# One hybrid decoder layer on one core: other part sizes in the third block's MLP, one norm at the end of the samples' attention, and a later place for the final norm's scaling

## The chip, the core and the metric

The kernel runs on one core of a Trainium2 chip. Time is device time in microseconds (us) of one execution, the median over the runs. A profile of one execution, taken by the hardware profiler, stands beside it: which instruction ran when on TensorE (PE, with its weight loads as PEld), VectorE (DVE), ScalarE (ACT), GpSimd (POOL), and what the DMA queue that SyncE (SP) issues did. In the profile's rows PEclk is the clock granted to TensorE, 1.00 being full speed.

## The reference

One inference step of one decoder layer, for a prompt of 2,048 tokens and for 64 sample tokens (8 sequences of 8, each with a paged cache of 2,048 past tokens), all in float32 with a model width of 1,024:

```
sh_m, sc_m, g_m, sh_f, sc_f, g_f = split(silu(c) @ w_ada + b_ada, 6)
h    = rmsnorm(x) * (1 + sc_m) + sh_m
rq, rk, rv, rg, sq, sk, sv = split(h @ w_in)        # 1024 -> 3584
ro   = groupnorm(retention(rotary(rq), rotary(rk), rv)) * silu(rg)   # 4 heads of 128
so   = stick_breaking_attention(sq, [past|sk], [past|sv])            # 8 heads of 64
so   = so * rsqrt(mean(so*so over each head) + eps) * sb_gn
x    = x + g_m * (concat(ro, so) @ w_out)
h    = rmsnorm(x) * (1 + sc_f) + sh_f
ff   = (silu(conv3(h @ w_up_gate)) * (h @ w_up_val)) @ w_down        # 1024 -> 2816 -> 1024
y    = rmsnorm_final(x + g_f * ff)
```

The outputs are y for prompt and samples, the new rows of k and v, the retention states and the last rows for the convolution.

## The kernel before

**Numbers.** Each float32 matrix product is done as three matmuls (L314, L315, L316) on a high and a low half of each operand, so that weights and activations are first split: an ACT cast writes the high half (L183, tile `whl` for weights, `act` for activations, `ahl` and `dmh` for attention results) and a DVE or POOL subtraction the low half (L165, which is the helper of all two-operand operations).

**Blocks.** The 2,048 tokens are worked in four blocks of 512, and each block in four tiles of 128. The 64 sample rows go with the fourth block (block number 3) through the MLP, as a fifth tile, which is then worked first. The MLP's inner width of 2,816 is 22 rows of 128.

**Stages.** First the modulation vectors; then the input projection of all four blocks, woven with the samples' attention (`decode`, L798 to L974); then the rest of the input projection with the samples' retention (`retention_sample`), the retention and the first block's attention; then, in the pool "mlp", the chain `mlps` (L1583): for each block `out_block` (output projection, residual, norm, and the `features` that bring the normed tiles into feature-major order, L1315) and then `ffn_block` (L1347). The attention of blocks 1 to 3 is woven into that chain. The last block's `ffn_block` runs alone, in the pool "mlp3".

**What sets the order.** The stages are Python generators. `_weave` takes the next step from the stream that is furthest behind its share of an assumed cost (1,230 for `mlps`, 420 for the attention there), so a moved `yield` moves work on every engine. A scheduler then orders the instructions of each engine; `tc.issue_after(x)` is a hint to it that what is issued under it comes after x. Small sets of buffers tie the engines together: six `whl` buffers (three pairs), two raw weight buffers, twelve `ff` buffers. The DMA loads and saves of all streams stand in one queue, SP's, in program order, and each waits there for its data or its buffer.

**The samples' attention, its end (L969 to L974).** `oT` holds the result as 4 x [128 features, 64 rows]. For each of the four, `sb_norm` (L450) squares it on ACT (L455), sums heads with small matmuls (L459), makes the reciprocal root in a chain of small POOL operations (tiles `sbr`, `sbms`), transposes it (L474), copies it out (L476), spreads it with a matmul against `sel4` (L479) and scales on DVE (L481). The result is split into `dmh`, of which there is one buffer, and saved to `mixs_sc` by one DMA each.

**The MLP (`ffn_block`, L1347).** It goes through `PARTS`, which are ranges of the 22 rows: 6, 6, 6 and 4. In each part the rows are made pair by pair (gate matmuls, a convolution of three taps, value matmuls, product, split into an `ff` tile), and then the part's share of the down projection is added, in two halves of 512 output columns. In the last part's second half two things are different. Ahead of it the next block's `out_block` is run (`after`, L1440). And the half's matmuls are done tile by tile (L1446 to L1456), with a step of the next block's `features` behind each tile, so that the matmuls of one tile cover the norm and modulation of the next block. Then come the weights of the next block's first gates, the residuals (L1459 to L1465) and `finish` (L1430), which is the final norm: square of the second half on ACT (L1432), reciprocal root on POOL (tile `rs_b`), scaling of one half on ACT (L1435) and of the other on DVE (L1436), and the DMA out. `finish` is a generator in two pieces, and a tile's second piece is called right behind the next tile's first.

## Time and profile before

| what | us |
|---|---|
| median of three runs | 3302.48 |
| the three runs | 3302.46, 3306.15, 3302.48 |
| the profiled execution | 3308.68 |
| span of the core in it, first to last instruction | 3307.0 |
| mean granted clock of TensorE in it | 0.986 |

| engine | busy us | share of the span | instructions |
|---|---|---|---|
| PE | 3187.8 | 96% | 17,879 |
| DVE | 2085.6 | 63% | 2,976 |
| ACT | 1580.0 | 48% | 2,796 |
| POOL | 1003.4 | 30% | 1,820 |

All stamps in the quoted rows are counted from the start of the span. A row of the wait view names the engine that waited, the tile and line that it was about to work on, and behind the arrow what ended the wait, then the total, the number of waits and the longest. A row of the window view gives for one stretch its length and the busy time (and number of instructions) of PE, PEld, DVE, ACT and POOL, then the granted clock, the share of the DMA engines and GB/s. A row of the groups gives busy time and mean ns of one instruction. A row of the timeline gives start, duration, engine, line and operation, and in brackets how long the engine had been idle and what released it.

### The profile page before, as it was taken

Reading aid. Unit: us, or ns where it says so; the run is one execution under the profiler, and the core shown is the slowest. Engines: PE = TensorE matmul, PEld = TensorE weight load, DVE = VectorE, ACT = ScalarE, POOL = GpSimd, SP = SyncE. Lnnn points to the kernel's source line nnn. Section 1 sums busy time; section 2 is a strip of 40 time slices with the busy share of each in tenths; the row PEclk is TensorE's granted clock in tenths of the full one; section 3 lists DMA queues with packets and bytes.
Section 4 is the critical chain, followed back from the end, with each engine's and each line's share of the span. In section 5 each row is a group of like instructions: output and inputs, shape, how many; then the busy total and the mean of one; then the engine's idle time right before and its main releaser. Section 6 shows DMA issues by size and latency. Waiting matters only on the chain. (4 is left out here: it accounts for less than half of the span.)

```text
span 3307.0 us, 50057 instructions
## 1 busy us (share of the span) xinstructions
PE 3187.8 (96%) x17879; PEld 2590.6 (78%) x17879; DVE 2085.6 (63%) x2976; ACT 1580.0 (48%) x2796; POOL 1003.4 (30%) x1820
## 2 busy tenths in 40 slices
PE   7999999999999989999999999999999999999998
PEld 5886777666878778878877778877788787799997
DVE  3345344245766587777778777787887874644445
ACT  4345335234534465545556555556655553533323
POOL 2012012013432243333344334344442433312112
PEclk8999999999999999999999999999999999999999
DMA  8757877785667744343454334354433335322321
GB/s 281 240 164 237 280 262 249 267 279 176 194 190 241 246 125 127 110 127 117 139 175 134 111 112 121 106 169 133 138 112 106 118 102 178 111 86 72 95 77 68
DMA packets 404135, 526.99 MB, mean 159 GB/s; under 512 B 25862, under 2 KB 242041, under 8 KB 403886
## 3 DMA queue, kind: packets, MB, share of 16 engines
q1 hardware_dynamic: 369966, 472.27, 45.6%
q10 hardware_dynamic: 33920, 51.52, 4.2%
q8 instruction: 142, 2.33, 0.3%
q14 instruction: 107, 0.88, 0.1%
HBM read 442.11 MB, written 81.60 MB: 158 GB/s over the span
## 5 line engine op out<-in xcount | busy, mean ns | idle before, releaser
L183 ACT CAST whl<-raw 128x1024 fp32r<-128x1024 f32 x408 | 427.6, 1050 | 1080.9 <-PE d L315 814.2
L165 DVE TENSOR_TENSOR whl<-raw,whl 128x1024 fp32r<-128x1024 f32 x408 | 521.6, 1280 | 571.8 <-ACT whl L183 561.6
L314 PE MATMUL d<-act,whl 128*128 128x512 f32 (+2 forms) x2016 | 742.9, 369 | 4.2 <-ACT whl L183 2.3
L316 PE MATMUL d<-act,whl 128*128 128x512 f32 (+2 forms) x2016 | 733.5, 364 | 0.0
L315 PE MATMUL d<-act,whl 128*128 128x512 f32 (+2 forms) x2016 | 731.4, 363 | 0.8 <-DVE act L165 0.8
L314 PEld LDWEIGHTS d<-act,whl 128*128 128x128 f32 x2016 | 382.8, 190 | 73.9 <-issue 12.0
L316 PEld LDWEIGHTS d<-act,whl 128*128 128x128 f32 x2016 | 382.1, 190 | 60.8 <-DVE whl L165 1.3
L315 PEld LDWEIGHTS d<-act,whl 128*128 128x128 f32 x2016 | 383.9, 190 | 55.8 <-DVE act L165 1.0
L314 PE MATMUL d<-whl,ff 128*128 128x512 f32 x704 | 279.6, 397 | 0.0
L315 PE MATMUL d<-whl,ff 128*128 128x512 f32 x704 | 278.7, 396 | 0.0
L316 PE MATMUL d<-whl,ff 128*128 128x512 f32 x704 | 278.1, 395 | 0.0
L314 PE MATMUL d<-whl,act 128*128 128x512 f32 x640 | 259.5, 407 | 4.0 <-ACT whl L183 4.0
L316 PE MATMUL d<-whl,act 128*128 128x512 f32 x640 | 258.3, 404 | 0.0
L315 PE MATMUL d<-whl,act 128*128 128x512 f32 x640 | 257.8, 403 | 0.0
L1181 DVE TENSOR_TENSOR_SCAN aom<-aom,acy 128x512 f32<-128x512 f32 x192 | 255.0, 1328 | 2.3 <-ACT aom L1167 1.7
L165 DVE TENSOR_TENSOR abe<-abe,aom 128x512 f32<-128x512 f32 (+2 forms) x320 | 230.5, 720 | 24.7 <-POOL abe L1171 2.5
L1205 PE MATMUL acc<-ahl,avv 128*128 128x512 f32 (+3 forms) x640 | 223.9, 411 | 12.0 <-DVE ahl L165 9.0
L1167 ACT ACTIVATE aom<-z,nb 128x512 f32<-128x512 f32 (+2 forms) x320 | 200.8, 628 | 62.8 <-PE z L1164 40.5
L1168 ACT ACTIVATE abe<-z,bb 128x512 f32<-128x512 f32 (+2 forms) x320 | 199.4, 623 | 0.7 <-DVE kf L165 0.7
L165 DVE TENSOR_TENSOR ahl<-z,ahl 128x512 fp32r<-128x512 f32 (+1 forms) x320 | 191.3, 598 | 10.9 <-ACT ahl L183 10.6
L1164 PE MATMUL z<-akk,aq 128*128 128x512 f32 (+3 forms) x640 | 190.1, 374 | 6.9 <-DVE ahl L165 3.1
L1374 DVE SCALAR_TENSOR_TENSOR c<-a,vecs,c 128x512 f32<-128x512 f32 x176 | 135.3, 769 | 80.8 <-ACT c L1371 46.1
(286 smaller groups left out, 5677.8 us busy)
## 6 DMA issues: line engine op xcount, KB each, us to landing
raw<-in_w_in SPq DMA_DIRECT2D x56, 1024.0 KB
raw<-in_w_up_gate SPq DMA_DIRECT2D x44, 1024.0 KB
raw<-in_w_up_val SPq DMA_DIRECT2D x44, 1024.0 KB
akk<-k SPq DMA_DIRECT2D x160, 256.0 KB
page<-in_cache_k_pages SPq DMA_DIRECT2D x128, 256.0 KB
vpage<-in_cache_v_pages SPq DMA_DIRECT2D x128, 256.0 KB
raw<-in_w_down SPq DMA_DIRECT2D x32, 1024.0 KB
raw<-in_w_ada SPq DMA_DIRECT2D x24, 1024.0 KB
```

Of the source, the lines that this page charges most:

```text
L165: eng.tensor_tensor(o, a, b, op)
L183: act.copy(hi, src)
L314: pe.matmul(ps, sh, mh, start=start, stop=False)
L315: pe.matmul(ps, sh, ml, start=False, stop=False)
L316: pe.matmul(ps, sl, mh, start=False, stop=stop)
L1164: pe.matmul(z[:, :n], qs[g, h][:, i * P : (i + 1) * P], kk[:, c, :n], start=c == 0, stop=c == 1)
L1167: act.activation(om[:, :n], z[:, :n], AF.Sigmoid, bias=nb[:, h : h + 1], scale=-SCALE)
L1168: act.activation(be[:, :n], z[:, :n], AF.Sigmoid, bias=bb[:, h : h + 1], scale=SCALE)
L1181: dve.tensor_tensor_scan(rv, rv, rv, init, ALU.mult, ALU.bypass)
L1205: pe.matmul(accs[0][:, cs], kv[u][1][:, kt, :], m[:, cs], start=(s == g and kt == 0 and c == 0), stop=(s == 0 and kt == NT - 1 and c == 1),)
L1374: dve.scalar_tensor_tensor(c[:, :TB], a[:, j : j + TB], cw(j), c[:, :TB], ALU.mult, ALU.add)
```

## The change

It has three parts. (1) The third block (number 2) gets parts of 6, 4, 4 and 8 rows instead of 6, 6, 6 and 4. The last part's second half begins with the rows but the last four, pair by pair over all tiles, with a step of `features` behind each pair, and does the last four rows tile by tile as before. For parts of four rows this loop is empty, so the other blocks keep their order. (2) At the end of the samples' attention one `sb_norm` over [128, 256] takes the place of four over [128, 64]: one square, two matmuls of the sums, two transposes, one copy, one `sel4` matmul, four scalings with a gain each, then one split into a `kh` tile and one DMA. (3) In `finish` the second piece of a tile is called two tiles behind, with the hint that it be issued behind the newest residual and square; the last two come behind the loop without a hint. This holds for all four blocks.

```
+LAST_PARTS = [(0, 6), (6, 10), (10, 14), (14, 22)]
...
-    def sb_norm(o, n, pl, gain, tag, rtag="sbsq", wait=0):
+    def sb_norm(o, n, pl, gains, tag, rtag="sbsq", wait=0, stag="sbsq"):
...
-        dve.scalar_tensor_tensor(out, o, gain, pb[:, :n], ALU.mult, ALU.mult)
+        w = n // len(gains)
+        for i, gain in enumerate(gains):
+            cs = slice(i * w, i * w + w)
+            dve.scalar_tensor_tensor(out[:, cs], o[:, cs], gain, pb[:, cs], ALU.mult, ALU.mult)
...
-        for j in range(4):
-            m = yield from steps(sb_norm(oT[:, j, :], NS, dp, vecs[:, V_SG + j : V_SG + j + 1], "dm"), 0.2)
-            mh = T(dp, [P, 2, NS], F32R, "dmh")
-            split(mh[:, 0], mh[:, 1], m)
-            sv(mixs_sc[4 + j], mh)
+        gains = [vecs[:, V_SG + j : V_SG + j + 1] for j in range(4)]
+        m = yield from steps(
+            sb_norm(oT.rearrange("p j t -> p (j t)"), 4 * NS, dp, gains, "aT", "aT", stag="aT"), 0.8
+        )
+        mh = T(dp, [P, 4, 2, NS], F32R, "kh")
+        split(mh[:, :, 0], mh[:, :, 1], m.rearrange("p (j t) -> p j t", j=4))
+        sv(mixs_sc[4:].rearrange("j p c n -> p j c n"), mh)
...
-        tt(eng, x2[:n, cs], x2[:n, cs], tmp[:n], ALU.add)
+        return eng.tensor_tensor(x2[:n, cs], x2[:n, cs], tmp[:n], ALU.add)
...
-                    wts = list(w_tm(w_dn, f0, f1 - f0, half * 512))
+                    wts = w_tm(w_dn, f0, f1 - f0, half * 512)
+                    for _ in range(f0, f1 - 4, 2):
+                        q0, w = next(wts)
+                        for q in range(2):
+                            for tile in ordered:
+                                one(pss, tile, f0 + q0 + q, w, q)
+                        yield cost / 2
+                        next(feats, None)
+                    wts = list(wts)
...
-                        residual(pss[tile[0]], gfs[half][tile[0] == NT], x2[tile[0]], half, tile[2], fp, dve)
+                        added = residual(pss[tile[0]], gfs[half][tile[0] == NT], x2[tile[0]], half, tile[2], fp, dve)
                         ends.append(finish(*tile, nf))
-                        next(ends[-1])
-                        if len(ends) > 1:
-                            next(ends[-2], None)
-                    next(ends[-1], None)
+                        squared = next(ends[-1])
+                        if len(ends) > 2:
+                            with tc.issue_after(added.ins), tc.issue_after(squared.ins):
+                                next(ends[-3], None)
+                    for end in ends[-2:]:
+                        next(end, None)
...
-                st = (yield from ffn_block(g, st, fp, False, nxt))[0]
+                st = (yield from ffn_block(g, st, fp, False, nxt, LAST_PARTS if g == 2 else PARTS))[0]
```

Lines behind the new constant move by one (L165 becomes L166, L183 becomes L184), and the residual's addition gets a line of its own (L1352); the scaling on DVE goes from L1436 to L1442.

Three places of the program show what moves. First SP, which issues the loads and saves, at the end of the samples' attention: `ms<-dmh` are the saves of the four norms' results, `raw` weights of the input projection, `rot` the rotary table, and the last four rows are loads of the retention stage behind. Before:

```order
L171 DMA raw_10078<-in_w_in 128x4x512
L171 DMA ms_148<-dmh_9643 128x128
L171 DMA rot_10485<-in_rot 128x2x512
L171 DMA raw_10221<-in_w_in 128x4x512
L171 DMA ms_148<-dmh_9670 128x128
L171 DMA ms_148<-dmh_9697 128x128
L171 DMA ms_148<-dmh_9758 128x128
L171 DMA c_decs_9797<-in_con 64x256
L171 DMA rv_9799<-rvs_114 64x512
L171 DMA rg_9801<-rgs_115 64x512
L171 DMA sqT_9804<-rqs_112 128x64
```

and now:

```order
L172 DMA raw_10002<-in_w_in 128x4x512
L172 DMA rot_10409<-in_rot 128x2x512
L172 DMA raw_10145<-in_w_in 128x4x512
L172 DMA ms_148<-kh_9682 128x4x128
L172 DMA c_decs_9721<-in_con 64x256
L172 DMA rv_9723<-rvs_114 64x512
L172 DMA rg_9725<-rgs_115 64x512
L172 DMA sqT_9728<-rqs_112 128x64
```

The saves, which stood between the weight loads and after them, have become one, `ms<-kh`, directly ahead of the retention's loads.

Second DVE between the third block's and the fourth block's MLP: `act<-hf` is the low half of a tile of the fourth block's features, `hf<-z` and `hf<-hf` their modulation, `whl<-raw` the low half of weights, `hf<-d` and `ff<-ff` the third block's residuals. Before:

```order
L165 TENSOR_TENSOR act_107_186<-hf_30639,act_107_186 128x4x128
L165 TENSOR_TENSOR whl_30735<-raw_30728,whl_30734 128x1024
L165 TENSOR_TENSOR act_107_186<-hf_30677,act_107_186 128x4x128
L165 TENSOR_TENSOR hf_30711<-z_30706,coef_102_168 128x512
L165 TENSOR_TENSOR hf_30711<-hf_30711,coef_103_169 128x512
L165 TENSOR_TENSOR whl_30943<-raw_30940,whl_30942 128x1024
L165 TENSOR_TENSOR act_107_186<-hf_30711,act_107_186 128x4x128
L165 TENSOR_TENSOR hf_30738<-d_30526,gp_25784 128x512
L165 TENSOR_TENSOR hf_30743<-d_30527,gp_25784 128x512
L165 TENSOR_TENSOR ff_24858<-ff_24858,hf_30738 128x512
L165 TENSOR_TENSOR ff_24861<-ff_24861,hf_30743 128x512
L165 TENSOR_TENSOR hf_30757<-d_30528,gp_25784 128x512
```

and now:

```order
L166 TENSOR_TENSOR whl_30651<-raw_30648,whl_30650 128x1024
L166 TENSOR_TENSOR act_107_186<-hf_30525,act_107_186 128x4x128
L166 TENSOR_TENSOR hf_30573<-z_30568,coef_102_168 128x512
L166 TENSOR_TENSOR hf_30573<-hf_30573,coef_103_169 128x512
L166 TENSOR_TENSOR act_107_186<-hf_30573,act_107_186 128x4x128
L166 TENSOR_TENSOR hf_30607<-z_30602,coef_102_168 128x512
L166 TENSOR_TENSOR hf_30658<-d_30388,gp_25708 128x512
L166 TENSOR_TENSOR hf_30607<-hf_30607,coef_103_169 128x512
L1352 TENSOR_TENSOR ff_24782<-ff_24782,hf_30658 128x512
L166 TENSOR_TENSOR hf_30663<-d_30389,gp_25708 128x512
L166 TENSOR_TENSOR act_107_186<-hf_30607,act_107_186 128x4x128
L1352 TENSOR_TENSOR ff_24785<-ff_24785,hf_30663 128x512
```

Before, the weights' low half stands ahead of the last tile's features and the residuals behind them; now two of the third block's residuals have moved in among the last two tiles' features.

Third DVE at the very end: `hf<-d` and `ff<-ff` are the residuals of the fourth block, and the rows that read `rs_b` are the final norm's scaling, of the samples (64x512) and of the four tiles. Before:

```order
L165 TENSOR_TENSOR hf_34809<-d_34717,gp_30802 128x512
L1436 SCALAR_TENSOR_TENSOR ff_34793<-ff_30234,rs_b_34803,gp_34714 64x512
L165 TENSOR_TENSOR ff_30225<-ff_30225,hf_34809 128x512
L1436 SCALAR_TENSOR_TENSOR ff_34798<-ff_30222,rs_b_34817,gp_34714 128x512
L165 TENSOR_TENSOR hf_34823<-d_34718,gp_30802 128x512
L1436 SCALAR_TENSOR_TENSOR ff_34812<-ff_30225,rs_b_34831,gp_34714 128x512
L165 TENSOR_TENSOR ff_30228<-ff_30228,hf_34823 128x512
L165 TENSOR_TENSOR hf_34837<-d_34719,gp_30802 128x512
L165 TENSOR_TENSOR ff_30231<-ff_30231,hf_34837 128x512
L1436 SCALAR_TENSOR_TENSOR ff_34826<-ff_30228,rs_b_34845,gp_34714 128x512
L1436 SCALAR_TENSOR_TENSOR ff_34840<-ff_30231,rs_b_34854,gp_34714 128x512
```

and now:

```order
L166 TENSOR_TENSOR hf_34720<-d_34637,gp_30722 128x512
L166 TENSOR_TENSOR hf_34734<-d_34638,gp_30722 128x512
L1352 TENSOR_TENSOR ff_30087<-ff_30087,hf_34720 128x512
L1442 SCALAR_TENSOR_TENSOR ff_34713<-ff_30096,rs_b_34728,gp_34634 64x512
L1352 TENSOR_TENSOR ff_30090<-ff_30090,hf_34734 128x512
L1442 SCALAR_TENSOR_TENSOR ff_34718<-ff_30084,rs_b_34742,gp_34634 128x512
L166 TENSOR_TENSOR hf_34748<-d_34639,gp_30722 128x512
L1442 SCALAR_TENSOR_TENSOR ff_34737<-ff_30090,rs_b_34765,gp_34634 128x512
L1352 TENSOR_TENSOR ff_30093<-ff_30093,hf_34748 128x512
L1442 SCALAR_TENSOR_TENSOR ff_34723<-ff_30087,rs_b_34756,gp_34634 128x512
L1442 SCALAR_TENSOR_TENSOR ff_34751<-ff_30093,rs_b_34774,gp_34634 128x512
```

Before, each scaling stands about one residual behind its own; now the residuals of the second and third tile stand ahead, with the samples' scaling between them, but the scaling of the third tile (`ff_34737`) is queued ahead of the last tile's addition, and that of the second tile behind it.

More of the change, by code (lines that the diff above doesn't have):

```diff
@@ L448, in to_features @@
             half_features(xs[kh], o, n, kh, A, B, acts[kh], hpool)
-    def sb_norm(o, n, pl, gain, tag, rtag="sbsq", wait=0):
+    def sb_norm(o, n, pl, gains, tag, rtag="sbsq", wait=0, stag="sbsq"):
         w = min(P, n)
         nt = n // w
-        sq = T(pl, [P, n], F32, "sbsq")
+        sq = T(pl, [P, n], F32, stag)
         act.activation(sq, o, AF.Square)
@@ L1218, in post @@
         def post(g, j, o2):
-            m = yield from sb_norm(o2, 512, tp, vecs[:, V_SG + j : V_SG + j + 1], "sbsq", *(("ahl", 1) if g else ()))
+            m = yield from sb_norm(o2, 512, tp, [vecs[:, V_SG + j : V_SG + j + 1]], "sbsq", *(("ahl", 1) if g else ()))
             mh = [T(tp, [P, 512], F32R, "ahl") for _ in range(2)]
@@ L1344, in residual, with ffn_block @@
         tt(dve, tmp[:n], fold(ps, n, fp)[:n], gate[:n, :], ALU.mult)
-        tt(eng, x2[:n, cs], x2[:n, cs], tmp[:n], ALU.add)
-    def ffn_block(g, x2, fp, samp, after=None):
+        return eng.tensor_tensor(x2[:n, cs], x2[:n, cs], tmp[:n], ALU.add)
+    def ffn_block(g, x2, fp, samp, after=None, parts=PARTS):
         t = TB + (NS if samp else 0)
@@ L1382, in gate @@
             return c
-        for f0, f1 in PARTS:
+        for f0, f1 in parts:
             ffs = {}
@@ L1431, in finish @@
                 y = T(fp, [P, 2 * t], F32, "ff")
-                act.activation(y[:n, :512], x2[i][:n, 512:], AF.Square, accum_out=ss[i][:n, 1:2])
-                yield
+                yield act.activation(y[:n, :512], x2[i][:n, 512:], AF.Square, accum_out=ss[i][:n, 1:2])
                 r = rows_rstd(ss[i], n)
@@ L1453, in ffn_block @@
                                 one(pss, tile, f0 + q0 + q, w, q)
-                        yield cost * (f1 - f0) / 4 / len(tiles)
+                        yield cost / len(tiles)
                         next(feats, None)
@@ L1544, in body @@
                 dict(smp=1, page=4, kh=4, vpage=6, aT=10, qsm=1, ksm=1, oT=1,
-                     tm=1, sbsq=1, dm=1, dmh=1, ptab=1, sbc=1, dbias=1, m8n=1, c_hm2=1, c_gsum=1),
+                     tm=1, ptab=1, sbc=1, dbias=1, m8n=1, c_hm2=1, c_gsum=1),
             )
```

## The prediction

> **What bounds the kernel now.** I read the page first, then the waits of TensorE, then the stretches around each place that the change touches.
>
> ```profile
> PE 3187.8 (96%) x17879; PEld 2590.6 (78%) x17879; DVE 2085.6 (63%) x2976; ACT 1580.0 (48%) x2796; POOL 1003.4 (30%) x1820
> PE   7999999999999989999999999999999999999998
> PEclk8999999999999999999999999999999999999999
> ```
>
> TensorE is busy 96% of the span, in every slice, and no other engine passes 63%. The change adds and removes almost no matmul work, so what it can win is the idle time of PE, 3307.0 − 3187.8 = 119.2 us in small gaps, and what else is lost where the granted clock is under 1. The three places touched are short stretches, so I cost each from its own window. All sums are made against the profiled execution, 3308.68 us (span 3307.0), which lies 6.2 above the median of 3302.48; since every term is a difference between two orders of the same work, I take the sum off the median unchanged. A measurement of this kernel tells some 0.2%, or 6.6 us, from nothing.
>
> **Part A, one norm at the end of the samples' attention.**
>
> ```profile
> PE z L474 <- POOL sbr L165: 2.8, 2, 1.5
> 744.00:747.00 3.00, 1.51 (x8) 0.90 (x7) 1.51 (x3) 1.15 (x2) 2.08 (x5) 1.00 0.02 9
> 747.00:757.00 10.00, 10.00 (x24) 6.16 (x25) 0.34 (x2) 0.66 (x3) 1.94 (x7) 0.51 0.34 112
> 757.00:767.00 10.00, 10.00 (x44) 8.02 (x43) 3.26 (x6) 3.57 (x6) 0.00 (x0) 0.98 0.19 56
> L479 PE MATMUL z<-sbsq,sel 4*128 4x64 f32 x4 | 1.4, 354 | 0.0
> L459 PE MATMUL z<-con,sbsq 128*64 128x2 f32 x8 | 1.2, 220 | 0.0
> L474 PE MATMUL z<-con,sbr 64*4 64x64 f32 x4 | 0.9, 227 | 2.8 <-POOL sbr L165 2.8
> ```
>
> The first row says that PE waited for the norms' POOL chain twice, 1.3 and 1.5 us. With one norm there is one such chain: the first wait stays, the second goes, 1.5 us. Behind the second wait the granted clock is 0.51 for ten microseconds (second window row), in which 24 matmuls were begun against 44 in the ten behind it. At the later rate these 24 take 24/44 × 10 = 5.5 us, so the slow stretch costs 4.5. I tie it to the second wait: PE was busy for half of the three microseconds ahead of it, and it begins where that thin stretch ends. The matmuls of the four norms take 1.4 + 1.2 + 0.9 = 3.5 us; one norm has one `sel4` matmul in place of four, two sums for eight and two transposes for four, so that some 1.5 are left and 2.0 go. Together 1.5 + 4.5 + 2.0 = **8.0 us**. Bounds: 3.5 if the clock falls anyway, and 9.4 if the first wait (1.3) goes too and 0.1 more of the norm's matmuls.
>
> What the new norm adds lies off PE, and the trace has no operation of just its size. The rows that bracket them:
>
> ```profile
> L455 ACT ACTIVATE sbsq<-o 128x512 f32<-128x512 f32 x16 | 10.1, 634 | 6.7 <-DVE o L165 6.6
> L455 ACT ACTIVATE sbsq<-oT 128x64 f32<-128x64 f32 x4 | 1.0, 257 | 7.0 <-DVE oT L934 4.0 <-PE z L479 3.0
> L479 PE MATMUL z<-ahl,sel 4*128 4x512 f32 x12 | 5.9, 493 | 0.0
> ```
>
> The square of 256 columns lies between 257 and 634 ns, and I take 0.38, between them in proportion. The `sel4` matmul lies between 354 and 493 ns, and I take 0.40. The wait that stays can thus grow by about 0.2 us, which I leave in the bounds. On SP the change goes past these:
>
> ```profile
> 746.76 16.02 SPq L171 DMA_DIRECT2D ms<-dmh  x3
> POOL km L1119 <- DMA sqT<-rqs: 15.8, 1, 15.8
> ```
>
> Three of the old saves blocked the queue for 16.02 us, because each needed the single `dmh` buffer, whose ACT casts stood behind a weight cast; POOL's first step of the retention stage waited 15.8 us for a load behind them. Now one save stands there, and those loads go some 15 us earlier. I cost this at nothing: PE has the input projection in hand meanwhile, in the window from 757 to 767 it is busy throughout, and that it goes on so is the cover; without it a rival (below) takes the 8 us back.
>
> **Part B, from the third block to the fourth.**
>
> ```profile
> PE z L314 <- ACT act L443: 5.1, 1, 5.1
> PE z L315 <- DVE act L165: 1.3, 1, 1.3
> PE z L420 <- DVE hf L165: 0.7, 1, 0.7
> PE z L420 <- ACT c L1324: 0.3, 1, 0.3
> 2860.00:2865.00 5.00, 0.07 (x1) 0.07 (x1) 4.97 (x6) 4.44 (x10) 1.84 (x2) 0.84 0.27 68
> 2865.00:2870.00 5.00, 3.69 (x14) 3.34 (x15) 5.00 (x7) 3.03 (x8) 1.87 (x4) 0.50 0.41 144
> 2870.00:2876.00 6.00, 6.00 (x46) 6.00 (x45) 3.29 (x6) 3.59 (x9) 3.25 (x8) 0.98 0.44 175
> 2842.64 0.40 PE L316 MATMUL d<-whl,act 128*128 128x512 f32 x1
> 2847.54 0.40 PE L316 MATMUL d<-whl,ff 128*128 128x512 f32 x1
> 2864.93 0.85 PE L314 MATMUL z<-act,whl 128*128 128x288 f32 x2 [5.08 <-ACT act L443]
> 2866.36 0.68 DVE L165 TENSOR_TENSOR act<-hf,act 128x512 fp32r<-128x512 f32 x1
> ```
>
> The first four rows are all the waits of PE from 2843 to 2876: 5.1 + 1.3 + 0.7 + 0.3 = 7.4 us. The first gate of the fourth block waits for the last tile's features. The 14 matmuls begun in the half-clock stretch (0.50) took 3.69 us; at the next row's 46/6 = 7.7 per us they take 1.8, so 1.9 more is lost. By the clock column the stretch at half lasts 0.16/0.5 × 5 + 5 + 0.02/0.5 × 6 = 6.8 us, and part A's 9.8 + 0.4 = 10.2: two and three steps of 3.4, in which I price such stretches. Now the cover. The features run as one chain from the last matmul of the output projection (2842.64) to the last split on DVE (2866.36 + 0.68 = 2867.04): 24.4 us. Against it PE has the half's matmuls and the transposes. From 2842.64 to 2847.54 are 21 steps of 0.233 us. Before, the last part has 4 rows × 4 tiles × 3 = 48 matmuls, 11.2 us; the features' transposes are what is left to 2864.93 − 5.08 = 2859.85: 17.2 less 11.2 less the small waits (1.0), 5.0. Now the part has 8 rows: 96 matmuls, 22.4 us, and 22.4 + 5.0 = 27.4 against 24.4. The gates then find their features, and 3.0 us are to spare. The extra 48 matmuls aren't added: they come out of the part of rows ahead of `out_block`. Of the waits I leave the 0.3 at the start: 7.4 − 0.3 + 1.9 = **9.0 us**. Bounds: 4 (if residuals that moved ahead of the last features on DVE delay them by as much as they spare, and the clock then falls for its 1.9) and 9.4.
>
> What these 48 matmuls leave behind is cover for the attention of the last block, whose end `out_block(3)` waits for:
>
> ```profile
> 2772.97 0.50 PE L479 MATMUL z<-ahl,sel 4*128 4x512 f32 x1
> 2776.86 0.34 SPq L171 DMA_DIRECT2D mx<-ahl  x1
> 2783.01 0.59 SPq L171 DMA_DIRECT2D smp<-ms  x1
> 2792.87 0.47 PE L323 MATMUL z<-whl,smp 128*128 128x512 f32 x1
> ```
>
> From the last `sel4` matmul to the save of its result on SP are 3.9 us, to the samples' load behind it 10.0, with its own 0.59 10.6; the samples' matmul came 19.9 behind. In the new order 24 matmuls (5.6 us, before 72) stand between that `sel4` matmul and the output projection, and the samples' matmuls come 34 matmuls further on: 14.0 us. So 14.0 against 10.6 is enough, and I cost it at nothing; the spare 3.4 us are about one weight load in SP's queue, and a rival has it.
>
> **Part C, the end.**
>
> ```profile
> 3296.34 0.75 DVE L1436 SCALAR_TENSOR_TENSOR ff<-ff,rs_b,gp 128x512 f32<-128x512 f32 x1 [1.20 <-POOL rs_b L165]
> 3298.34 0.69 DVE L165 TENSOR_TENSOR ff<-ff,hf 128x512 f32<-128x512 f32 x1
> 3300.02 0.75 DVE L1436 SCALAR_TENSOR_TENSOR ff<-ff,rs_b,gp 128x512 f32<-128x512 f32 x1 [1.00 <-POOL rs_b L165]
> 3302.57 0.75 DVE L1436 SCALAR_TENSOR_TENSOR ff<-ff,rs_b,gp 128x512 f32<-128x512 f32 x1 [1.80 <-POOL rs_b L165]
> 3300.65 0.61 ACT L1432 ACTIVATE ff<-ff 128x512 f32<-128x512 f32 x1
> 3301.43 0.19 POOL L165 TENSOR_TENSOR sst<-os 128x1 f32<-128x1 f32 x1 [1.45 <-ACT ff L1432]
> 3301.99 0.55 POOL L165 TENSOR_TENSOR rs_b<-rs_a,nhalf 128x1 f32<-128x1 f32 x1
> ```
>
> The last addition ends at 3299.03, but its square begins only at 3300.65, because ACT has the third tile's scaling queued ahead; square to scaling then takes 3300.65 to 3303.32. Two things win. The last addition comes earlier, since the second tile's scaling, which waited 1.20 and took 0.75, is no longer ahead of it; the third tile's still is, in the order shown above, so of this 1.95 I take 1.6: it ends near 3297.4. And its square follows at once, 0.8 with the read of its sum; POOL's chain (3301.43 to 3302.54) takes 1.1, the scaling 0.75, with small passages 2.9: 3300.3 instead of 3303.32. That is **3.0 us**; bounds 1.9 (one of the two) and 3.3.
>
> **Part D, the same rescheduling between blocks 0, 1 and 2.**
>
> ```profile
> PE acc L1205 <- DVE ahl L165: 1.6, 1, 1.6
> PE acc L1205 <- DVE ahl L165: 2.1, 1, 2.1
> ```
>
> These are the longest waits of PE from 1720 to 1790 and from 2290 to 2350: attention splits on DVE that stand behind a waiting scaling. If the scalings no longer wait there, 3.7 us go; something else will often be late next, so I take half, **2.0 us**, with bounds of 0 and 5.4 (3.7 and half of a clock step of 3.4).
>
> **Sum.** 8.0 + 9.0 + 3.0 + 2.0 = 22.0; 3308.68 − 22.0 = 3286.7, on the median 3302.48 − 22.0 = **3280.5 us**.
>
> **A rule weighed.** The row at 747 shows half clock behind a wait of 1.5 us. The Trainium skill, "TensorE: Matmul & The Clock Gate", sections "What's actually happening" and "HAM oscillation — how this bites in real kernels", says that the gate halves the clock after an idle window of some 3.4 us, in windows that run free of the program. By that rule a 1.5 us wait doesn't make the slow stretch, part A would be worth 3.5 and the sum 17.5. The trace agrees for B, where 5.1 us of wait stand ahead of the stretch, and speaks against it in A.
>
> **The rivals.**
>
> *The slow clock at 747 stays.* A thin stretch remains (fewer, but still dependent small matmuls and the wait of 1.3), and the clock falls behind that wait instead. A is 3.5: 3285.0. For it: the wait that stays is nearly as long as the one that goes (1.3 and 1.5). Against: before, behind the first wait the window from 744 still shows 1.00. Chance 0.14.
>
> *The output projection waits for the last attention row.* If a weight load (3.6 us) holds SP's queue between that row's saves, PE waits some 4 us ahead of the fourth block, and the clock falls for one or two steps of 3.4 us at half, 1.7 to 3.4. That takes 5.7 to 7.4 of B's 9.0: about 3288. For it: only 3.4 us to spare. Against: both saves are queued early. Chance 0.13.
>
> *A is given back.* The retention stage, whose loads come 15 us earlier, draws work on DVE and ACT forward, and the input projection's splits come later: the 8.0 goes, 3288.5. Chance 0.09. With the rival before it, 3288.5 + 7.4, about 3296: within 0.2%. Chance 0.05.
>
> *Slower, by the phase of the clock.*
>
> ```profile
> 1150.00:1200.00 50.00, 41.91 (x235) 35.69 (x236) 42.07 (x58) 34.46 (x69) 19.63 (x42) 0.86 0.38 110
> ```
>
> Here a clock of 0.86 means 0.14/0.5 × 50 = 14 us at half, 7 lost. Everything behind 745 moves by 8 us, and with it where each small gap lies against the steps of the clock. If gaps that now pass unpunished draw such stretches, each 7 us at worst, four take back 22 + 6.6 = 28.6: that is the point from which it is slower; five give 3302.5 − 22 + 35 = 3315.5. For it: most of the 119 us are small gaps. Against: as many stretches may vanish. Chance 0.03.
>
> **How the numbers follow.** The forecast has 0.56, the rivals 0.14, 0.13, 0.09, 0.05 and 0.03. Faster: 0.56 + 0.14 + 0.13 + 0.09 = 0.92; same 0.05; slower 0.03. Downward the range reaches 9.4 + 9.4 + 3.3 + 5.4 = 27.5 and some 2 of clock elsewhere: 3273. Upward it takes in the three faster rivals with 3 us for the bounds of C and D: 3292. Outside are the last two and little else.
>
> **What would show it.** Right: no second wait of the transposes of `sbr` near 745 and a clock near 1 from 747 to 757; one save there, and `km` no longer waiting; the first gate of the fourth block without a wait of its own above 1 us and no half clock behind it; the last square right behind the last addition, and the last scaling three microseconds nearer to it. Wrong: a new wait of `d` matmuls for `act` or `smp` loads ahead of the fourth block's output projection; the slow stretch still behind the single norm; or gaps in the retention stage that were not there.

## The result, and the profile after

| kernel | median us | runs | before beside it | ratio to before, 95% interval |
|---|---|---|---|---|
| changed | 3286.24 | 6 | 3305.95 | 0.9945 [0.9934, 0.9956] |
| changed, measured again (`after_again`) | 3284.13 | 6 | 3304.84 | 0.9933 [0.9910, 0.9956] |

The change makes the kernel faster, by 0.0055 × 3305.95 = 18.2 us in the first measurement and 0.0067 × 3304.84 = 22.1 in the second; 22.0 were forecast. In time, 3280.5 us were forecast and 3286.24 and 3284.13 measured; 3.5 and 2.4 us of that distance are there because before itself ran slower beside the change (3305.95 and 3304.84) than the 3302.48 from which the forecast was taken. The profiled execution took 3287.1 us with a span of 3285.4, 21.6 under that of before. First the page, its totals and clock:

```profile
PE 3175.4 (97%) x17870; PEld 2584.1 (79%) x17870; DVE 2084.3 (63%) x2970; ACT 1577.2 (48%) x2787; POOL 999.9 (30%) x1805
PEclk8999999999999999999999999999999999999999
```

PE is busy 12.4 us less, with nine matmuls fewer, and idle 110.0 us, 9.2 less. So more than half of what this trace gains isn't idle time: it is matmuls that don't run at half clock, and the norm's small ones. Not all of it is the change's, as the next table shows.

**Where it came from, stage by stage.** All kernels here split the same 408 weight pieces on DVE (`whl<-raw`). The start of the n-th split, counted from 0, is a milestone; the table has the time in the trace of before, and for each other trace how much later (earlier where negative) it is there. The end is that of the last scaling on DVE.

| milestone | before, us | changed | again | A only | B only | C only | `smp_first` | `best` |
|---|---|---|---|---|---|---|---|---|
| 78, ahead of the norms | 735.8 | -3.9 | -0.9 | -1.7 | -3.1 | -1.6 | +3.3 | -5.2 |
| 88, retention begun | 843.7 | -11.0 | -12.1 | -14.2 | -3.8 | -4.2 | -9.0 | -17.9 |
| 190, ahead of 0→1 | 1691.6 | -11.6 | -14.1 | -13.9 | -3.5 | -2.5 | -9.4 | -19.7 |
| 202, behind 0→1 | 1797.1 | -12.4 | -14.8 | -14.2 | -3.3 | -3.2 | -10.2 | -21.8 |
| 265, ahead of 1→2 | 2270.2 | -12.5 | -14.9 | -14.2 | -3.4 | -3.2 | -10.2 | -21.7 |
| 276, behind 1→2 | 2368.7 | -14.3 | -16.7 | -15.8 | -3.3 | -5.0 | -12.0 | -22.9 |
| 330, ahead of 2→3 | 2767.9 | -13.7 | -16.2 | -15.7 | -2.7 | -4.9 | -11.4 | -22.3 |
| 350, behind 2→3 | 2909.8 | -20.0 | -25.2 | -14.6 | -8.5 | -4.3 | -21.3 | -32.2 |
| 405, ahead of the end | 3262.2 | -20.0 | -25.1 | -14.6 | -8.5 | -4.3 | -21.2 | -32.1 |
| end | 3303.3 | -22.5 | -27.7 | -14.6 | -8.5 | -6.9 | -23.8 | -35.6 |

Two things are seen in it. Up to the first milestone every trace has the instructions of before in the same order, and yet they lie from -5.2 to +3.3 (`six_rows`, which the table leaves out, at -5.6): 8.9 us from one execution to another, as much as a term of the forecast, so only differences between milestones are read. And the time changes at the places of the change and moves by at most 2.0 us between them.

**A, the norm.** The waits of PE from 730 to 760, the two windows that stood at half clock and at full speed in before, and SP's save:

```profile
PE z L476 <- POOL sbr L166: 1.3, 1, 1.3
```
```profile
747.00:757.00 10.00, 10.00 (x51) 7.36 (x50) 3.07 (x5) 2.22 (x3) 1.12 (x3) 1.00 0.97 235
757.00:767.00 10.00, 9.34 (x50) 6.60 (x49) 4.86 (x10) 6.21 (x16) 2.58 (x9) 1.00 0.74 217
```
```profile
741.51 0.46 SPq L172 DMA_DIRECT2D ms<-kh  x1
...
743.97 0.58 SPq L172 DMA_DIRECT2D sqT<-rqs  x1
```

One wait of 1.3 is left, 51 matmuls are begun where 24 were, at clock 1.00, and the save takes 0.46 us where three blocked the queue for 16.02. The load `sqT` is issued at 743.97 and not at 765.37. But the wait that was to go with it stays; POOL's row from 730 to 860:

```profile
POOL km L1126 <- DMA sqT<-rqs: 14.2, 2, 13.9
```

The longest was 15.8 before and is 13.9 now. POOL's step ahead of that copy, the zeroing of `km`, comes earlier too (734.76, before 751.55), so POOL waits nearly as long as it did.

**B, the third block to the fourth.** The waits of PE from 2740 to 2900, and the two rows around the longer one:

```profile
PE z L324 <- DMA smp<-ms: 1.8, 1, 1.8
PE z L421 <- ACT c L1331: 0.3, 1, 0.3
```
```profile
2773.05 0.40 PE L315 MATMUL d<-whl,act 128*128 128x512 f32 x1
2775.29 0.47 PE L324 MATMUL z<-whl,smp 128*128 128x512 f32 x1 [1.85 <-DMA smp<-ms]
```

The waits of 5.1, 1.3 and 0.7 for the features are gone, only the 0.3 that was to stay has stayed. In their place stands a new one, 1.8 us for the samples' load, ahead of the fourth block's output projection, and behind it the clock falls:

```profile
2775.00:2780.00 5.00, 4.71 (x14) 3.79 (x15) 1.23 (x1) 1.05 (x1) 0.00 (x0) 0.68 1.04 363
```

14 matmuls in five microseconds at a clock of 0.68.

**C, the end.** DVE's last rows:

```profile
3274.86 0.68 DVE L166 TENSOR_TENSOR hf<-d,gp 128x512 f32<-128x512 f32 x1
3276.73 0.75 DVE L1442 SCALAR_TENSOR_TENSOR ff<-ff,rs_b,gp 128x512 f32<-128x512 f32 x1 [1.18 <-POOL rs_b L166]
3277.40 0.68 DVE L1352 TENSOR_TENSOR ff<-ff,hf 128x512 f32<-128x512 f32 x1
3278.00 0.74 DVE L1442 SCALAR_TENSOR_TENSOR ff<-ff,rs_b,gp 128x512 f32<-128x512 f32 x1
3280.06 0.75 DVE L1442 SCALAR_TENSOR_TENSOR ff<-ff,rs_b,gp 128x512 f32<-128x512 f32 x1 [1.31 <-POOL rs_b L166]
```

From the end of the last addition (3278.08) to that of the last scaling (3280.81) are 2.7 us; before, 4.3. The last addition itself still waits behind the third tile's scaling, as the order had shown.

### The profile page after: what moved, and what is told of

Same layout as the page of the kernel before. It is cut to its first block, busy times and chain, and to the rows that moved or that the text cites. A ratio compares the mean times of both kernels' runs of the same rounds, so it can differ in the third digit from the quotient of the medians.

```text
span 3285.4 us, 49997 instructions
## 1 busy us (share of the span) xinstructions
PE 3175.4 (97%) x17870; PEld 2584.1 (79%) x17870; DVE 2084.3 (63%) x2970; ACT 1577.2 (48%) x2787; POOL 999.9 (30%) x1805
## 5 line engine op out<-in xcount | busy, mean ns | idle before, releaser
L184 ACT CAST whl<-raw 128x1024 fp32r<-128x1024 f32 x408 | 427.6, 1050 | 1091.7 <-PE d L316 825.7
L166 DVE TENSOR_TENSOR whl<-raw,whl 128x1024 fp32r<-128x1024 f32 x408 | 521.7, 1280 | 560.7 <-ACT whl L184 551.9
L166 DVE TENSOR_TENSOR abe<-abe,aom 128x512 f32<-128x512 f32 (+2 forms) x320 | 231.3, 723 | 24.7 <-POOL abe L1178 2.5
L166 DVE TENSOR_TENSOR ahl<-z,ahl 128x512 fp32r<-128x512 f32 (+1 forms) x320 | 191.3, 598 | 7.9 <-ACT ahl L184 7.5
L1352 POOL TENSOR_TENSOR ff<-ff,hf 128x512 f32<-128x512 f32 (+1 forms) x101 | 161.7, 1630 | 84.8 <-DVE hf L166 84.1
```

The costliest lines, as they stand in the source:

```text
L166: eng.tensor_tensor(o, a, b, op)
L184: act.copy(hi, src)
L1352: return eng.tensor_tensor(x2[:n, cs], x2[:n, cs], tmp[:n], ALU.add)
```

## The experiments

Each is timed against before on the same chip; the columns of the table above and the tables here give what its trace shows.

**The three parts alone.** `a_only`, `b_only` and `c_only` are the kernel before with the lines of one part of the change each.

> The kernel before with part A alone, the one norm at the end of the samples' attention. My theory: the weight splits behind the norms come 7.7 us earlier against those just ahead of them (in the changed kernel's trace the shift goes from -3.3 at 727 us to -11.0 at 825), the clock from 747 to 757 is near 1, and the median falls by 8 us. Rival one: the 3.3 us by which the changed kernel is early already at 700 us belong to part A too (other buffers in that pool), then it falls by 11. Rival two: the half-speed stretch behind the norms comes and goes from run to run and is not tied to the second wait; then this trace may show it again and the gain is 3.5.

> The kernel before with part B alone, the third block's parts of 6, 4, 4 and 8 rows. My theory: the waits of the fourth block's first gates go (8.4 us with the clock behind them), but the samples' matmuls of the output projection wait for the load smp by 1.8 us and half a clock step of 3.4 us follows, 1.7: net 5.5 to 6.5 us faster. Rival: the wait for smp is an accident of one run; then 9 faster.

> The kernel before with part C and D alone, the later place of the final norm's scaling. My theory: 2.5 us at the end and 2 us at the two transitions between blocks 0, 1 and 2: 4.5 faster, half of it in waits of acc matmuls for ahl near 1770 and 2335. Rival: the transitions give nothing of their own (what the changed trace shows there is the phase of other things), then 2.5.

| run | median us | ratio to before (3306.52), 95% interval | us by the ratio |
|---|---|---|---|
| `a_only` | 3295.70 | 0.9963 [0.9949, 0.9978] | -12.2 |
| `b_only` | 3296.96 | 0.9971 [0.9958, 0.9985] | -9.6 |
| `c_only` | 3303.29 | 0.9988 [0.9976, 0.9999] | -4.0 |

Each part is faster by itself, C by little: its interval ends at 0.9999. Together they would give 25.8, with an uncertainty of some 8; the whole gave 18.2 and 22.1, which isn't apart from it. The 3.3 us that the changed kernel was early at 700 us are not part A's: B alone, which changes nothing there, has -3.1 at the first milestone and A alone -1.7. That rival is out.

For A I split the stretch of the norms (milestones 78 to 80) and the one behind it (80 to 88) into what the clock costs, (1 - granted clock) × length, and the rest:

| trace | norms | 78 to 80: clock + rest | 80 to 88: clock + rest |
|---|---|---|---|
| before | four | 5.1 + 18.0 | 3.4 + 81.4 |
| `c_only` | four | 1.6 + 18.6 | 1.7 + 83.5 |
| `b_only` | four | 3.5 + 18.2 | 1.7 + 83.9 |
| `saves_act` | four, saves on ACT | 1.7 + 19.4 | 5.1 + 79.5 |
| `norms_inter` | four, side by side | 5.2 + 16.4 | 1.7 + 82.4 |
| `a_only` | one | 0 + 13.8 | 1.6 + 80.0 |
| changed | one | 0 + 13.8 | 7.0 + 80.0 |
| changed again | one | 0 + 13.8 | 1.7 + 81.3 |
| `smp_first` | one | 0 + 13.8 | 1.6 + 80.2 |
| `six_rows` | one | 0 + 13.8 | 1.7 + 81.1 |
| `best` | one | 0 + 13.8 | 1.6 + 79.8 |
| `best_again` | one | 0 + 13.8 | 7.0 + 80.4 |

What the clock costs comes in steps: 1.7, 3.4, 5.1 and 7.0, give or take 0.1, are nearly one to four times 1.7, which is what the prediction's step of 3.4 us at half clock costs. In the stretch with four norms the clock falls in all five traces, in that with one in none of seven. But how long it stays down changes from one execution to the next, with the same two waits in it in before, `c_only` and `b_only`. Their windows from 740 to 760, in this order:

```profile
740.00:760.00 20.00, 18.51 (x59) 11.95 (x60) 3.64 (x10) 3.50 (x9) 5.42 (x17) 0.74 0.32 99
```
```profile
740.00:760.00 20.00, 18.49 (x71) 12.38 (x70) 4.05 (x11) 4.80 (x11) 4.45 (x15) 0.91 0.32 99
```
```profile
740.00:760.00 20.00, 18.49 (x71) 12.45 (x70) 4.11 (x11) 4.80 (x11) 4.02 (x12) 0.91 0.26 83
```

0.74 once and 0.91 twice; `b_only` has a second stretch at half clock ahead of this window, from 736.2 to 739.6, behind the first wait. So the prediction's 4.5 us were those of one execution; over the three traces with this code it is 3.4.

**The load of the samples' rows first (`smp_first`).** On the changed kernel:

```
...
+        if samp:
+            loaded = ld(smp, mixs_sc.rearrange("k p c n -> p k c n"))
         for k in range(KT):
             ld(acts[k // 4][:, k % 4, :, :TB], mix_sc[g][k])
-        if samp:
-            ld(smp, mixs_sc.rearrange("k p c n -> p k c n"))
...
             if samp:
-                gates.append(load_g(0, 0, fp, xpool))
+                with tc.issue_after(loaded.ins):
+                    gates.append(load_g(0, 0, fp, xpool))
```

> The changed kernel with one thing more: the load of the samples' rows (smp) for the fourth block's output projection is queued directly behind the last attention save, ahead of the last act load and ahead of the gp load that holds the queue for 3.6 us. My theory: in the changed kernel the wait of 1.8 us for smp and the half clock from 2775 to 2778 are lost for want of this; here both go, 3.5 us faster than the changed kernel, 22 to 23 under the kernel before. Rival one: the load lands late because the DMA engines are full (share 1.05 in that stretch), not because it is issued late: then the wait stays above 1 us. Rival two: now the act rows come late and PE waits for those by as much: no change.

It takes 3283.57, ratio 0.9924 [0.9908, 0.9940]; the changed kernel had 0.9945 and 0.9933, and the intervals overlap, so that what follows rests on the traces. SP's rows around the load, first of the changed kernel, then of this one:

```profile
2762.27 0.37 SPq L172 DMA_DIRECT2D mx<-ahl  x1
...
2767.90 0.53 SPq L172 DMA_DIRECT2D act<-mx  x1
2768.48 0.59 SPq L172 DMA_DIRECT2D smp<-ms  x1
```
```profile
2764.61 0.38 SPq L172 DMA_DIRECT2D mx<-ahl  x1
2765.03 0.42 SPq L172 DMA_DIRECT2D smp<-ms  x1
2770.43 0.53 SPq L172 DMA_DIRECT2D act<-mx  x1
```

The load went out 6.2 us behind the last save, now 0.4: it no longer stands behind a `gp` load that went out only at 2766.34. In the waits of this kernel from 2740 to 2890 one row is left, 0.3 us for `c`; none for `smp`, and none for the act rows, though these are issued later than before. Both rivals are out. From milestone 330 to 350 it gains 9.9 us on before, where the changed kernel gained 6.3 with a wait of 1.8, its second trace 9.0 with one of 0.7, and `b_only` 5.8 with one of 2.3:

```profile
PE z L324 <- DMA smp<-ms: 0.7, 1, 0.7
```
```profile
PE z L324 <- DMA smp<-ms: 2.3, 1, 2.3
```

The wait is no accident of one run: it stands in all three traces of that order, and its length changes.

**Six rows in the last part (`six_rows`).** On `smp_first`, `LAST_PARTS = [(0, 6), (6, 12), (12, 16), (16, 22)]`.

> The changed kernel with the samples' load moved as in the run smp_first, and parts of 6, 6, 4 and 6 rows in the third block. The last part's half then covers the fourth block's features with 72 matmuls of 0.2335 us and 5.0 of transposes: 21.8 us against a chain of 24.4. Theory: the first gates of the fourth block wait 2.6 us, and 0 to 1.7 go to the clock: 2.5 to 4.5 slower than smp_first. Rival: the cover isn't what counts in this place but where the weights' split stands on DVE; then no wait, or one as long as before (5.1 and 1.3).

It takes 3285.36, ratio 0.9941 [0.9926, 0.9955]. By the ratios that is some 6 us more than `smp_first`, with intervals that overlap, and the profiled execution was the fastest of its four (3278.49). In the traces it is 1.3 us longer than `smp_first` from 330 to 350 (133.4 against 132.1), and its waits from 2735 to 2885 are:

```profile
PE d L315 <- DVE hf L166: 1.1, 1, 1.1
PE z L421 <- ACT c L1332: 0.3, 1, 0.3
```

Less than the 2.5 that I expected, and for something else: the wait for the features (`act`) does not come back, the 1.1 us are for a `d` bank that a residual on DVE (`hf`) had not yet read. The features' chain isn't shorter here: from the last matmul of the output projection (2817.24) to the end of the last split it takes 27.7 us, and in the changed kernel 26.3 (2821.00 to 2847.28), not the 24.4 of before. What fills the time is work that I had overlooked. The first gates are 48 matmuls into `d` and 48 into `z`, and here those into `d` go first. Two rows of PE, and between them the last split on DVE:

```profile
2840.27 0.40 PE L315 MATMUL d<-act,whl 128*128 128x288 f32 x1 [1.14 <-DVE hf L166]
2843.19 1.78 DVE L166 TENSOR_TENSOR act<-hf,act 128x512 fp32r<-128x512 f32 x1
2846.78 0.29 PE L315 MATMUL z<-act,whl 128*128 128x288 f32 x1
```

Those into `d` begin 2.9 us ahead of the last split and so don't need it; they take 6.5 us and cover the rest of the chain. In before, PE had seven of the matmuls into `z` in front, waited there 5.1 and 1.3 us, and only then came to those into `d`:

```profile
2868.45 0.44 PE L314 MATMUL d<-act,whl 128*128 128x288 f32 x1
```

This order stands in all five traces without part B, and `d` first in all seven with more rows in the last part. So 48 matmuls of cover and the worse order always come together, and no run parts them. Behind before's wait for the features stood 48 matmuls that take 6.4 us at its later rate (0.133 us each); how many of them could have run in that wait isn't shown, so how much of the 7.1 us is the longer cover's and how much the order's stays open.

**Saves from another queue (`saves_act`).** On the kernel before:

```
-            sv(mixs_sc[4 + j], mh)
+            sva(mixs_sc[4 + j], mh)
```

> The kernel before with one edit: the four saves at the end of the samples' attention are issued from ACT's queue and not SP's, so that the retention's loads behind them on SP aren't held for 16 us. Norms, matmuls and waits stay. In the first traces the stretch behind the norms (from the weight split 80 to 88) is 81 to 84 us long without part A and 80 with it, when half of the half-clock time is taken off. Theory: part of A's gain is that SP is freed, then here this stretch is 80 and the wait of km is gone, while the stretch with the norms (78 to 80) stays at 18.0 to 18.6 plus what the clock costs. Rival: SP was covered, as the prediction said; then 82 to 84. For the clock: the same two waits of PE stand here again; if half clock behind them is a matter of the execution, its length differs again from the 10.2 us of before.

It takes 3304.70, ratio 0.9993 [0.9981, 1.0005]: no change that can be told from none. In its trace the stretch from 80 to 88 is 79.5 without the clock's share, as short as with one norm (80.4 in the mean of seven) and shorter than in the three traces with SP held (82.9 in the mean); against it the norms' own stretch grew by 1.1. The wait of `km` for `sqT` here and, for comparison, in `b_only`:

```profile
POOL km L1119 <- DMA sqT<-rqs: 4.2, 2, 2.4
```
```profile
POOL km L1120 <- DMA sqT<-rqs: 14.4, 2, 13.4
```

The wait of `km` is no measure of this, since the changed kernel keeps it (14.2), and here POOL waits 13.6 us at the next step instead, until PE's `acc` matmuls have read the buffer. So the trace speaks for SP: the start of the retention stage is 2 to 4 us shorter with the queue free, which I had costed at nothing. It isn't shown: the median doesn't have it, and PE's own waits in the stretch are 6.1 here and 5.8 to 7.7 with one norm, but 6.3, 9.0 and 8.7 in before, `c_only` and `b_only`, where before held SP the longest.

The clock answers the other question of this run. Its first two waits (a third, of 0.83, follows at 752.07) and two windows of it:

```profile
737.43 0.21 PE L474 MATMUL z<-con,sbr 64*4 64x64 f32 x1 [1.31 <-POOL sbr L165]
748.15 0.21 PE L474 MATMUL z<-con,sbr 64*4 64x64 f32 x1 [1.28 <-POOL sbr L165]
```
```profile
738.00:740.00 2.00, 2.00 (x6) 1.14 (x4) 0.00 (x0) 0.00 (x0) 0.60 (x1) 0.50 0.40 61
748.00:756.00 8.00, 7.02 (x28) 4.63 (x29) 0.86 (x4) 1.17 (x5) 2.29 (x9) 1.00 0.61 189
```

Here half clock stands behind the first wait and full clock behind the second, the other way round than in before; in `b_only` it stands behind both. It isn't the second wait by itself that draws the stretch; and since the one norm has that first wait of 1.3 too and never a fall behind it, neither does the first alone.

**Four norms side by side (`norms_inter`).** On the kernel before, with buffers of the tags `aT` and `kh`:

```
+        norms = [sb_norm(oT[:, j, :], NS, dp, ...) for j in range(4)]
+        for _ in range(3):
+            for norm in norms:
+                next(norm)
+            yield 0.2
...
```

> The kernel before with the four norms kept, but stepped side by side: all four squares, then all four sums, and so on. As many matmuls and ACT and DVE instructions as before, but one POOL chain to wait for (four times as long in POOL's own work). Theory: the wait counts. PE waits once, 1.3 us plus up to 3 x 0.5 for the longer chain, no half clock behind it, and the stretch from the weight split 78 to 80, 18.0 to 18.6 before without the clock's share and 13.8 with one norm, is 16 to 17; in all 5 to 9 faster. Rival: the thin stretch of small matmuls draws the half clock, wait or no wait; then 78 to 80 still loses 1.7 to 5 to the clock.

This one missed. It takes 3320.31, ratio 1.0040 [1.0026, 1.0054], slower by 13 us. PE's waits from 736 to 757.5:

```profile
PE z L474 <- POOL sbr L165: 3.8, 3, 2.5
```

There are three waits, 3.8 us in all, since POOL works the four chains one behind the other; so the run doesn't take the waits away and can't tell them from the thin stretch of small matmuls: half clock (0.50 to 0.84 in the windows from 738 to 750) follows the longest. What draws it stays open between the two. SP is free in this run too (its four saves take 1.76 us), and yet the stretch from 80 to 88 is 82.4 without the clock, as long as with SP held; it has another order of work as well, so this is no clean test of SP. And the rest of the loss lies elsewhere: the weaving has four steps here where it had twelve, which is probably why later work comes in another order, and from 842 to 1140 PE waits on things that it doesn't wait on in before:

```profile
PE z L1016 <- DVE on L1008: 5.2, 8, 1.8
PE z L1175 <- DVE scd L165: 4.2, 2, 3.0
PE z L474 <- DVE rmh L165: 2.9, 1, 2.9
```

Its trace ends only 4.6 us behind that of before (3311.6 against 3307.0 in the span), because the two executions aren't typical: this one took 3313.27, 7.0 under its median, and that of before 3308.68, 3.3 above the median measured beside this run.

**Load first and last scalings last (`best`, twice).** On `smp_first`:

```
-                    for end in ends[-2:]:
-                        next(end, None)
+                    with tc.issue_after(added.ins), tc.issue_after(squared.ins):
+                        for end in ends[-2:]:
+                            next(end, None)
```

> The run smp_first with one thing more: the last two tiles' scalings at the very end are also issued behind the last residual and square. On DVE the third tile's scaling then no longer stands ahead of the last tile's addition. In the changed kernel that scaling waited 1.18 and took 0.75 ahead of it. Theory: the last addition ends 1.9 earlier, the last square follows it, and the end comes 1.9 earlier: 5 us under the changed kernel, 24 to 25 under the kernel before. Rival: POOL's chains, one behind the other at 1.4 us each, become what the last scaling waits for; then 1 us or less.

It takes 3283.02, ratio 0.9935 [0.9922, 0.9947]. DVE's last rows, and POOL's last one:

```profile
3262.70 0.68 DVE L166 TENSOR_TENSOR hf<-d,gp 128x512 f32<-128x512 f32 x1
3263.42 0.69 DVE L1353 TENSOR_TENSOR ff<-ff,hf 128x512 f32<-128x512 f32 x1
3264.03 0.74 DVE L1443 SCALAR_TENSOR_TENSOR ff<-ff,rs_b,gp 128x512 f32<-128x512 f32 x1
3265.49 0.75 DVE L1443 SCALAR_TENSOR_TENSOR ff<-ff,rs_b,gp 128x512 f32<-128x512 f32 x1 [0.72 <-POOL rs_b L166]
3266.97 0.75 DVE L1443 SCALAR_TENSOR_TENSOR ff<-ff,rs_b,gp 128x512 f32<-128x512 f32 x1 [0.72 <-POOL rs_b L166]
```
```profile
3266.38 0.55 POOL L166 TENSOR_TENSOR rs_b<-rs_a,nhalf 128x1 f32<-128x1 f32 x1
```

The last addition now follows its product at once, but the last two scalings come 1.5 us apart, each behind its chain on POOL. The end gains 0.9 us (milestone 405 to the end: 3.5 against 2.6), not 1.9: the rival was right, POOL's chains are late next. The new hint holds for all four blocks: in both traces of `best` the transition 0→1 gains 2.1 where the changed kernel gained 0.7 or 0.8, and 1→2 gains 1.0 or 1.2 where it gained 1.8.

> The changed kernel once more, unaltered, side by side with the next run. The three parts alone gave ratios to before of 0.9963, 0.9971 and 0.9988, which make 0.9922 together, and the whole gave 0.9945 in its first measurement. Theory: the parts add, and the first trace had a half-clock stretch of some 10 us from 760 to 800 that the runs with the same norm elsewhere don't have; then this ratio lies near 0.993 and the trace loses under 4 us to the clock between the weight splits 80 and 88, against 7.0. Rival: the parts take something from each other; then 0.9945 again and the same loss in the same place.

> The run best once more, unaltered: the changed kernel with the samples' load queued first and the last scalings behind the last residual. Theory: 3.5 us from the load and 0.9 from the end, 4.4 under the changed kernel measured beside it (ratio to before 0.9935 in its first measurement). Rival: the wait for the load was small in most executions of the changed kernel and the profiled one was unlucky; then 0.9 to 2 under it.

Side by side, the changed kernel took 3284.13, ratio 0.9933 [0.9910, 0.9956], and `best` 3280.89, ratio 0.9917 [0.9897, 0.9937]. The 3.2 us between the medians lie between the 4.4 expected and the rival's 2, and the intervals overlap: in both measurements `best` has the lower median, but that it beats the change is likely, not shown. The loss to the clock from 80 to 88 was 1.7 in the repeat, against 7.0. Where the first trace lost it, two windows of it and the same two stretches of the second trace, which runs some 3 us later there:

```profile
770.00:776.50 6.50, 4.98 (x25) 3.39 (x25) 4.41 (x8) 4.59 (x10) 3.85 (x8) 1.00 0.86 232
776.50:787.00 10.50, 10.50 (x29) 6.22 (x27) 5.07 (x8) 5.15 (x8) 3.11 (x9) 0.51 0.46 140
```
```profile
773.00:779.50 6.50, 5.56 (x30) 3.94 (x28) 4.55 (x8) 4.58 (x10) 3.85 (x8) 1.00 0.84 236
779.50:790.00 10.50, 10.50 (x49) 7.43 (x48) 6.46 (x9) 6.41 (x12) 3.35 (x9) 1.00 0.76 228
```

The program is the same, and the clock is 0.51 in one and 1.00 in the other. The stretch at half speed begins behind a wait of PE for `ssc`, 1.5 us in the first trace and 0.9 in the second. `best` and `best_again`, one program too, have 0.9 and 1.5 there and lost 1.6 and 7.0; but before, `b_only`, `c_only` and `six_rows` have 1.5 as well and lost 1.7 to 3.4, so the wait alone doesn't decide it.

## Why the prediction was right, point by point

**The whole.** 22.0 were forecast, 18.2 and 22.1 measured. By the milestones A gives 9.5, B 6.3 and 9.0, C 2.6 and D 1.9: the sum came out nearly as forecast, but not each term for its reason: A gave more than forecast, B and C as much or less. Of the signs named beforehand two failed: `km` still waits 13.9 us, and the last scaling came 1.6 us nearer to the last addition, where three were named (the forecast's own sum makes 1.4). One sign of being wrong came, a wait for `smp`.

**A: 8.0 forecast, 9.5 by the traces.** One wait is left, and there is no half clock with the one norm, as forecast; but the step "I tie it to the second wait" failed, since `saves_act` has its half clock behind the first. What the change takes away is four norms' worth of short waits and small matmuls in a row, in which the clock falls at one place or another. The stretch of the norms is 18.3 - 13.8 = 4.5 us shorter without the clock (3.5 forecast, 1.5 of wait and 2.0 of matmuls; the matmuls gave 2.2, from 3.5 to 1.3, with four rows of sums left in the trace and not two), and 3.4 shorter by the clock (4.5 forecast, from one execution). The stretch behind, which I had costed at nothing, is 82.9 - 80.4 = 2.5 shorter, and loses 3.2 - 2.3 = 0.9 more to the clock. That SP's free queue is the cause of the 2.5 is likely by `saves_act` (79.5) and not shown: `norms_inter` has a free queue and 82.4, and the longest hold, that of before, goes with the shortest stretch of the three (81.4). 4.5 + 3.4 + 2.5 - 0.9 = 9.5. The rival by which the clock stays down at 747 is out, seven traces of seven. The rule of the Trainium skill that was weighed ("TensorE: Matmul & The Clock Gate", section "What's actually happening": half clock after an idle window of some 3.4 us) doesn't give these falls: the waits ahead of them are 1.3 to 1.5 us, and 2.5 in `norms_inter`.

**B: 9.0 forecast, 6.3 and 9.0 measured, 9.9 without the wait for the samples** (the four other traces without part B are 0.6 to 1.3 longer here than before, so these are, if anything, low). The cover came out as reckoned: 27.3 us from the last matmul of the output projection to the first new gate (2848.33), against 27.4, and no wait for the features is left. But the chain grew with it, to 26.3 from 24.4, so that 1.0 was to spare and not 3.0; and the 7.4 us of waits may not have been for want of cover alone, as I had read them: PE had gates that waited for the last tile ahead of 48 that, by `six_rows`, don't need it. The share of each is open. The step that failed in the time is "14.0 against 10.6 is enough". In the 10.6 the samples' load counted with its own 0.59 us, which is the time that its issue takes on SP, not that of its bytes. From `sel4` (2759.22) to the issue (2768.48) were 9.3 us, where 10.0 were reckoned; but PE could begin only at 2775.29, 6.8 behind the issue, with the DMA engines' share at 0.91 in that time. (In the second trace and in `b_only` it began 5.7 and 7.2 behind.) 16.1 against 14.0 makes a wait of 2, and 1.85 stands in the row. The rival of the output projection that waits has thus come in part: its place was right, its mechanism (a weight load between the saves) was not, and its price was 0.7 to 2.3 us of wait with up to 1.7 of clock (3.4 us at half), not 5.7 to 7.4.

**C: 3.0 forecast, 2.5 to 2.6 measured** (changed -20.0 to -22.5, again -25.1 to -27.7, alone -4.3 to -6.9). From the last addition to the end, 1.6 were won (4.3 less 2.7) where 1.4 were forecast (4.3 less 2.9). The last addition comes 0.9 to 1.0 earlier in its stage and not 1.6: the third tile's scaling ahead of it waits 1.18, where the one that left had waited 1.20.

**D: 2.0 forecast, 1.9 by the milestones**, but not through the waits that I had added up. With part C the two transitions gain 0.7 or 0.8 and 1.8 in each of four traces (changed, again, C alone, `smp_first`), 2.5 in the mean. Without it they gain 0 in `b_only` and `saves_act`, but 1.8 in `a_only` and `norms_inter`: with before 0.7 in the mean. At 0→1 the gain is part C's: the wait of 1.6 near 1770 stands in `a_only`, `b_only` and `saves_act` as in before, and with part C it did shrink:

```profile
PE acc L1212 <- DVE ahl L166: 0.7, 1, 0.7
```

At 1→2 that isn't shown. The wait near 2335 is 2.1 in before, 1.3 in `b_only`, which has no part C, and 2.3 in `c_only`, which has it. And the 1.8 that `c_only` gains there are the clock: it has one stretch of 3.4 us at half clock where before has two (at 2313.9 and 2348.0). What gives the 1.8 in the other three, and 1.5 to 1.6 in `a_only` and `norms_inter` without part C, stays open.

**The slower rival, the phase of the clock.** Its mechanism is real: the same program loses 7.0 us to the clock from milestone 80 to 88 in one execution and 1.7 in another, as the windows from 770 to 790 show. But it falls to both sides, and differs between executions of one kernel more than between kernels: it spreads the runs (3276.6 to 3292.6 for the changed kernel) and doesn't move the median by 28. The Trainium skill, "TensorE: Matmul & The Clock Gate", section "What's actually happening", says that the gate's window runs free of the program, and that the cost at a kernel's start therefore varies from run to run. The traces here agree as far as they go, with 0.51 and 1.00 in the same stretch of one program, though in the middle of the kernel.

**The chain from the trace of one execution.** The forecast took from the median what one trace had shown. Repeated traces of the unchanged first 735 us differ by up to 8.9 us; that the sum came out is also luck: in the two terms (A's clock, D's waits) whose sources differ from one execution to the next, and in that A's excess and B's new wait fell to opposite sides.

## What to carry to other kernels

When work is moved to cover one chain, look at what the same work had covered where it stood, and there count a DMA from its issue to the use of its bytes in a stretch with the queues as full as they will be, not by its issue on the queue: here 0.59 against 6.8 us. Before a wait is put down to missing cover, look whether the waiting engine has work behind it that could have gone first: here 48 matmuls, 6.4 us. A half-clock stretch or a short wait that one profile shows is a sample; cost it by several traces, or by any stretch of the same kernel that other experiments leave alone. Where waits are taken from the end of a chain, work out the next engine's own rate first: POOL's 1.5 us for each tile set the end when DVE no longer did.

## What the runs showed of the hardware that I had not expected

The granted clock of the same stretch of the same program, some 10 us without idle time of PE, was 0.51 in one execution, behind a wait of 1.5 us, and 1.00 in another, behind one of 0.9. And a load of the samples' rows (512 KB) took 6.8 us from its issue to the first matmul that used it while the DMA engines' share was 0.91.
